# Row buffers of 4096 bytes and pads in a transformer block's kernel

## The chip, the cores and the metric

The kernel runs on one core of one Trainium2 chip, as one program. The metric is device time in microseconds from launch to end, the median of three runs: 1248.03 (1245.07 to 1248.34). One further execution was profiled and took 1247.24 us; every time read from the trace belongs to it.

## What is computed

One layer of a block with 1024 latent tokens and 256 context tokens of width 1024. The reference, cut:

```python
px = modulate(rms_norm(x, g_pre_mix), sh_m, sc_m) @ w_in       # 1024 tokens
pc = modulate(rms_norm(ctx, g_pre_mix), csh_m, csc_m) @ w_in   # 256 context tokens
att_x = window_attention(qx, kx, vx, kc, vc, sink)             # 8 query heads, 2 key heads, band 128
h_ml_x, _, _ = mlstm_bidir(xq, xk, xv, xg, st_f, st_b)         # 4 heads, both directions
mix_x = concatenate([att_x, ml_x], -1) @ w_out
x = x + gt_m * rms_norm(mix_x, g_post_mix)
fx = (silu(h @ w_gate) * (h @ w_up)) @ w_ffn_out               # h: x normed, modulated; hidden 2816
x = x + gt_f * rms_norm(fx, g_post_ffn)
```

The shifts, scales and gates are products of a conditioning vector with the six parts of w_ada.

## The kernel before

All data is float32. A product of two float32 operands is made of three matmuls in the type float32r: each operand is split into a rounded part (hi, copied by ScalarE, L59) and the rest (lo, subtracted by VectorE, L60), and `mm3` (L68) issues hi·hi, hi·lo and lo·hi as lines 71 to 73. In the terms of the code the first operand of a matmul is the stationary one, loaded into TensorE as weights (PEld in the profile), and the second moves past it. The moving operand is mostly 512 columns wide, 2048 bytes of a partition; the stationary one 128 columns, 512 bytes.

The stages, with their times in the profiled execution:

- 0 to 50 us: shift and scale from w_ada (L209). Norm, transposition and split of the tokens begin here (`prep_a`, `prep_b`).
- 50 to 92: gates, attention values and the first mLSTM head (`s1`, slabs of 272 columns of w_in, moving operand w1, stationary hh, hl or ch, cl).
- 92 to 133: the other three mLSTM value heads (slabs of 384 columns, L392, moving w2). `gates` (L303) and `ml_weights` (L378) run beside it.
- 133 to 309: thirteen weight tiles of w_in (`tproj`, L427, lines 438, 439, 441; stationary th and tl in R, moving hh, hl). Convolutions, rotary, the remaining w_ada parts (`ada_rest`, L479; sums over the partitions L499, L505) and the mLSTM state steps (`state_step`, L531) run between them.
- 309 to 498: attention and mLSTM outputs, item by item after a written plan (L35, L36).
- 498 to 600: output projection row by row (`omm`, L883; stationary mh and ml, moving woh and wol in R), norms, transposition, split into b11 to b22.
- 600 to 1009: gate and up products. The 2816 hidden columns go in 22 steps p by a scheme of seven products for each two-by-two block (`fm`, L1163). Each product is 12 matmuls, so a step is 84. Products 1, 2 and 3 have b11, b21, b22 moving; products 6, 5, 7 and 4 have T2, T1, T3, T4 (tT in the profile), which lie in R.
- 1009 to 1245: down projection by the same scheme (`fmm`, L1434; both operands are in one buffer fo), 924 matmuls.

From L873 on the order of the instructions of each engine is written out by hand; before it a planner places them. All DMAs are issued from SP's queue, in program order.

**Where the buffers lie.** Pools are opened as a stack: one from the low end of each partition's memory, another (side right) from the high end. Their buffers follow each other with starts at multiples of 32 bytes, so the sizes fix where each begins. The function `R` (L119) hands out sixteen row buffers, r0 to r15, that many stages share; each is RW = 1032 floats, 4128 bytes, which is eight times 512 and 32 more. They lie in the order of their first use: r0 to r3, r8 to r13, r6, r4, r7, r14, r15, r5. The remainders of the starting addresses modulo 512, worked out from the sizes:

| buffers | remainder modulo 512 |
|---|---|
| hh, hl (tokens), later mix | 480 |
| r0 to r3 (ch, cl; states; woh, wol; T3) | 352, 384, 416, 448 |
| r8 to r13 | 480, 0, 32, 64, 96, 128 |
| r6, r4, r7, r14, r15, r5 | 160, 192, 224, 256, 288, 320 |
| th, tl (in r9, r10 and r11, r12) | 0, 32 and 64, 96 |
| V; av2 | 352; 0 |
| w1h, w1l (rows of 1088 bytes) | 256 or 0 |
| w2h, w2l | 0 |
| k2, qh and ql | 256, 320 |
| probabilities split for the values product (th_, tl_) | 0 |
| mh, ml; b11 to b22; wg; wS and w22; fo | 352 |

A slice of 128 or 512 columns begins a multiple of 512 bytes into its buffer, so it has the buffer's remainder. The rows of V and of the mLSTM states have 129 floats, 516 bytes, so their slices do not. A buffer that is opened over released ones waits for the last use of those that it overlaps (`reuse_waits="tile"`).

Of the kernel before, what the change touches and what calls it, by code (L numbers as in the profile page):

```python
# [9 lines left out]
F32 = mybir.dt.float32  # L10
F32R = mybir.dt.float32r
# [5 lines left out]
P = 128  # L17
# [13 lines left out]
NCONST = 576  # L31
VSIL, VCONV, VGML, VBADA, VGPM, VGPF = 0, 16, 28, 32, 64, 72
NVEC = 80
RW = 1032
PLAN_ML = "T0 q A0 A1 A2 A3 T1 T2 T3 M0 M1 T4 V0 N0 M2 V1 M3 M4 O z V2 w V3 s N1 x"  # L35
PLAN = "T0 q A0 A1 A2 A3 T1 T2 T3 N0 M0 T4 M1 M2 N1 M3 M4 O z l"  # L36

# [1 line left out]
def body(tc, x, ctx, vecs, bcv, bada, gqm, gqf, wada, ws1, ws2, wt, wout, wfi, wfo,  # L39
# [5 lines left out]
    def open_pool(name, bufs=1, side="left", space=None):  # L45
        kw = dict(name=name, bufs=bufs, reuse_waits="tile")
        if space is not None:
            kw["space"] = space
        else:
            kw["side"] = side  # L50
        p = tc.tile_pool(**kw)
        return p, p.__enter__()
# [32 lines left out]
    c = cp[1]  # L85
# [11 lines left out]
    hcol = c.tile([P, 2, KT], F32, name="hcol")  # L97
    sfc = c.tile([P, KT], F32, name="sfc")
    hfc = c.tile([P, KT], F32, name="hfc")
    dma(vec, vecs)  # L100
    pool.memset(epst, EPS)
    pool.memset(one, 1.0)
# [14 lines left out]
    rp = open_pool("R")  # L117

    def R(k, name, shape, dt=F32):  # L119
        t = rp[1].tile([P, RW], dt, name=name, tag=f"r{k}")  # L120
        n = int(np.prod(shape))
        v = t[:, 0:n]
        if len(shape) == 2:
            v = v.rearrange("p (a b) -> p a b", b=shape[1])
        elif len(shape) == 3:
            v = v.rearrange("p (a b c) -> p a b c", b=shape[1], c=shape[2])
        elif len(shape) == 4:
            v = v.rearrange("p (a b c d) -> p a b c d", b=shape[1], c=shape[2], d=shape[3])
        return v


    vp = open_pool("V")
    V = vp[1].tile([P, NT, 4, 129], F32, name="V")
    Vc = vp[1].tile([P, NC_, 4, 129], F32, name="Vc")
    av2 = vp[1].tile([P, NT + NC_, 4, 64], F32R, name="av2")
    G = vp[1].tile([P, 4, 16, 4], F32, name="G")
    pool.memset(V[:, :, :, 128:129], 1.0)
# [7 lines left out]
    hh = [htp[1].tile([P, 4, S], F32R, name=f"hh{i}") for i in range(2)]  # L145
    hl = [htp[1].tile([P, 4, S], F32R, name=f"hl{i}") for i in range(2)]
    ch = [R(i, f"ch{i}", (4, L), F32R) for i in range(2)]
    cl = [R(2 + i, f"cl{i}", (4, L), F32R) for i in range(2)]
    gp = open_pool("gcol")
    ucol = gp[1].tile([P, P], F32, name="ucol")  # L150
    emcol = gp[1].tile([P, P], F32, name="emcol")
    wkcol = gp[1].tile([P, P], F32, name="wkcol")
    decb = gp[1].tile([P, 64], F32, name="decb")
    a_d = tc.dram_tile([P, P], F32, name="a_d")
    w_d = tc.dram_tile([P, P], F32, name="w_d")
    p1 = open_pool("p1")
    q1 = p1[1]
    w1h = [q1.tile([P, 4, 272], F32R, name=f"w1h{i}") for i in range(2)]
    w1l = [q1.tile([P, 4, 272], F32R, name=f"w1l{i}") for i in range(2)]

    cs4 = q1.tile([P, KT, 4], F32R, name="cs4")
    cz4 = q1.tile([P, KT, 4], F32, name="cz4")
    split(cs4[:, :, 0:2], cs4[:, :, 2:4], csil)
# [13 lines left out]
    def prep_a(i):  # L177

        j = i - NT
        xt = xts[i] = R(4 + i % 4, f"xt{i}", (D,))  # L180
        xd[i] = dma(xt, x[i * P:(i + 1) * P] if i < NT else ctx[j * P:(j + 1) * P])
        hraw[i] = R((12, 13, 8, 9, 10, 11)[i % 6], f"hraw{i}", (KT, P))
        act.activation(hraw[i].rearrange("p a b -> p (a b)"), xt, AF.Square, accum_out=st[:, i:i + 1])
        rms_r(st[:, 10 + i:11 + i], st[:, i:i + 1])
        pool.tensor_scalar(xt, xt, st[:, 10 + i:11 + i], 1.0, MUL, MUL)
# [23 lines left out]
    for sec in (1, 0):  # L209
# [30 lines left out]
        for q in range(2):  # L240
            t = (hcol, scol)[sec][:, q]
# [157 lines left out]
    akp = open_pool("ak")  # L399
    k2 = [akp[1].tile([P, S + L], F32R, name=f"k2_{g}") for g in range(2)]  # L400
    c1t = [akp[1].tile([P, 2, 129], F32, name=f"c1t{d}") for d in range(2)]
    p2 = open_pool("p2")
    q2 = p2[1]
    mk = [R(4 + i, f"mk{i}", (S,)) for i in range(2)]
# [10 lines left out]
    def T(i, name):  # L415
        return q2.tile([P, S], F32, name=name, tag=f"s{i}")
# [169 lines left out]
    for j, name in enumerate(TILES):  # L586
# [5 lines left out]
        i = int(name[-1]) if name[-1].isdigit() else 0  # L592
# [4 lines left out]
        elif name == "ak":  # L597
# [5 lines left out]
            for a, b, w, dst in ((kr, ks, S, slice(0, S)), (kc[:, 0:L], kc[:, L:2 * L], L, slice(S, S + L))):  # L603
                t = th[64:P] if w == S else kc[64:P, 2 * L:3 * L]
# [7 lines left out]
        elif name.startswith("aq"):  # L612
            t = T(0, f"aq{i}")
# [3 lines left out]
        else:  # L617
            t = R(14 if i == 3 else 15, "so", (S,))
# [23 lines left out]
        if 0 <= j - 3 < 9:  # L642
            s_ = j - 3
            if s_ >= 1 and s_ % 2 == 1:
                k = (s_ - 1) // 2
# [12 lines left out]
    mix = [mixt[:, n] for n in range(NT)]  # L658
    atp = open_pool("att")
    qa = atp[1]  # L660

    def bank():
        return pb.tile([P, 4, P], F32, name="pt", tag="pt", bufs=3)
# [787 lines left out]
    for p in range(4, HT):  # L1451
# [41 lines left out]
        else:  # L1493
            X4 += two_banks()
            t = pb.tile([P, D], F32, name="fx2", tag="s", bufs=2)
# [85 lines left out]
    for s_ in range(1, 8):  # L1581
        q0 = (s_ - 1) * NJ
        KL = 4 if s_ == 7 else 2
        if s_ == 2:
            t = pb.tile([P, D], F32, name="fy0", tag="s", bufs=2)
# [121 lines left out]
```

## Time and profile before

| what | us |
|---|---|
| median of three runs | 1248.03 |
| profiled execution | 1247.24 |
| its span, first to last instruction | 1245.4 |
| TensorE busy (PE) | 1205.8 |
| VectorE busy (DVE) | 799.9 |
| ScalarE busy (ACT) | 580.1 |
| GpSimd busy (POOL) | 204.0 |

In the trace a row of a group has the line, the engine, the operation, what is written and read by the program's names (numbers left out), the shape, the count, the busy time in us and the mean of one in ns, and after the last bar the idle time before them with what ended it. The records of neighbouring matmuls overlap: a record reaches from a matmul's start to the end of its last result. The rate is the step from one start to the next.

### The profile page before, as it was taken

What the parts mean: (1) busy time and instruction counts of PE and PEld (TensorE: products, weight loads), DVE (VectorE), ACT (ScalarE), POOL (GpSimd) and SP (SyncE); (2) the same over time, 40 slices, a digit from 0 to 9 for tenths busy, and PEclk for the clock granted to TensorE, in tenths of its full rate; (3) what the DMA queues carried; (4) which work ended last, traced back from release to release, by engine and by line L of the source; (5) the groups of instructions that cost most, each with busy time, mean ns of one, the idle gap of its engine ahead of it and who ended that gap; (6) DMA issues with size and microseconds to landing.
All of it is one profiled execution on the core that took longest, in us unless ns stands there. A gap on an engine that the chain in (4) does not pass through costs nothing.

```text
span 1245.4 us, 16232 instructions
## 1 busy us (share of the span) xinstructions
PE 1205.8 (97%) x5859; PEld 971.7 (78%) x5859; DVE 799.9 (64%) x1375; ACT 580.1 (47%) x1111; POOL 204.0 (16%) x245
## 2 busy tenths in 40 slices
PE   7889999999999998999899999999999999999997
PEld 1779887877777786888678888888888878888885
DVE  3882268763877787355867677767776655554566
ACT  3754533111666796677633333333333325434542
POOL 0752401244644475000000000000000000000000
PEclk9899999999999999999999999999999999999999
DMA  8532855655422320522033465665644547665853
GB/s 310 173 123 73 300 164 152 186 147 197 121 85 86 114 74 9 203 81 72 17 104 140 162 220 189 216 237 191 216 144 169 180 160 268 203 212 187 308 172 118
DMA packets 90952, 201.78 MB, mean 162 GB/s; under 512 B 9076, under 2 KB 29940, under 8 KB 89464
## 3 DMA queue, kind: packets, MB, share of 16 engines
q1 hardware_dynamic: 90872, 200.74, 48.1%
q8 instruction: 46, 0.75, 0.2%
q14 instruction: 34, 0.28, 0.1%
HBM read 149.32 MB, written 50.73 MB: 161 GB/s over the span
## 4 chain that ended last, share of the span: by engine, by line
PE 74%; DVE 9%; DMA 7%; ACT 4%; POOL 2%; issue 2%; SPq 1%; DVEq 0%; POOLq 0%; ACTq 0%
PE xv L72 7%; PE xv L71 7%; PE xv L73 7%; PE pt L72 5%; PE pt L71 5%; PE pt L73 5%; PE pt L704 2%; PE pt L703 2%; PE pt L804 2%; DMA wb<-in_wada 2%; PE t L438 2%; PE t L441 2%; PE t L439 2%; PE s L774 1%; PE op L71 1%
## 5 line engine op out<-in xcount | busy, mean ns | idle before, releaser
L60 DVE TENSOR_TENSOR fo<-fr,fo 128x1024 fp32r<-128x1024 f32 x77 | 92.7, 1222 | 71.4 <-ACT fo L59 68.4
L59 ACT CAST fo<-fr 128x1024 fp32r<-128x1024 f32 x77 | 79.6, 1051 | 74.0 <-PE pt L73 36.5
L438 PE MATMUL t<-hh,th 128*128 128x512 f32 x208 | 83.4, 401 | 0.9 <-ACT cr L455 0.9
L439 PE MATMUL t<-hl,th 128*128 128x512 f32 x208 | 82.6, 397 | 0.0
L59 ACT CAST wS<-wr 128x512 fp32r<-128x512 f32 x88 | 54.1, 622 | 57.9 <-PE pt L73 38.0
L60 DVE TENSOR_TENSOR wS<-wr,wS 128x512 fp32r<-128x512 f32 x88 | 60.4, 688 | 20.8 <-ACT wS L59 20.7
L71 PE MATMUL xv<-tT,wS 128*128 128x512 f32 x168 | 67.7, 403 | 3.7 <-ACT tT L1079 2.0
L441 PE MATMUL t<-hh,tl 128*128 128x512 f32 x208 | 68.6, 394 | 0.0
L72 PE MATMUL xv<-tT,wS 128*128 128x512 f32 x168 | 67.6, 402 | 0.0
L73 PE MATMUL xv<-tT,wS 128*128 128x512 f32 x168 | 66.6, 397 | 0.3 <-DVE wS L60 0.3
L489 DVE SCALAR_TENSOR_TENSOR acc<-wb,csil,acc 128x1024 f32<-128x1024 f32 x24 | 34.4, 1433 | 39.4 <-DMA wb<-in_wada 39.2
L438 PEld LDWEIGHTS t<-hh,th 128*128 128x128 f32 x208 | 39.1, 188 | 10.1 <-ACT cr L455 1.3
L940 DVE TENSOR_TENSOR wr<-wr 128x512 f32<-128x512 f32 x66 | 45.5, 689 | 1.5
L439 PEld LDWEIGHTS t<-hl,th 128*128 128x128 f32 x208 | 39.1, 188 | 8.4 <-issue 1.2
L1191 ACT ACTIVATE es<-es 128x512 f32<-128x512 f32 x22 | 13.9, 632 | 67.6 <-DVE es L943 67.6
L441 PEld LDWEIGHTS t<-hh,tl 128*128 128x128 f32 x208 | 38.2, 188 | 8.5 <-issue 1.0
L71 PE MATMUL op<-woh,mh 128*128 128x512 f32 x112 | 44.7, 399 | 0.0
L72 PE MATMUL op<-wol,mh 128*128 128x512 f32 x112 | 44.2, 394 | 0.0
L73 PE MATMUL op<-woh,ml 128*128 128x512 f32 x112 | 44.1, 394 | 0.0
L774 PE MATMUL s<-k,qh 128*128 128x256 f32 (+1 forms) x128 | 41.5, 335 | 1.9 <-ACT so L620 1.0
L71 PE MATMUL pt<-fo 128*128 128x512 f32 x110 | 42.8, 389 | 0.0
L72 PE MATMUL pt<-fo 128*128 128x512 f32 x110 | 42.8, 389 | 0.0
(982 smaller groups left out, 3498.1 us busy)
## 6 DMA issues: line engine op xcount, KB each, us to landing
wr<-in_wfi SPq DMA_DIRECT2D x44, 512.0 KB, 5.0
wb<-in_wada SPq DMA_DIRECT2D x24, 512.0 KB, 4.1
s_d<-a SPq DMA_DIRECT2D x22, 512.0 KB, 6.5
bt<-in_wfo SPq DMA_DIRECT2D x44, 256.0 KB, 4.0
tb_d<-bt SPq DMA_DIRECT2D x11, 1024.0 KB, 3.9
fr<-s_d SPq DMA_DIRECT2D x44, 256.0 KB, 3.5
fr<-tb_d SPq DMA_DIRECT2D x44, 256.0 KB, 4.6
fr<-a_d SPq DMA_DIRECT2D x33, 256.0 KB, 4.3
```

Source lines behind the costliest of these rows:

```text
L59: act.copy(hi, raw)
L60: dve.tensor_tensor(lo, raw, hi.bitcast(F32), SUB)
L71: pe.matmul(ps, a[0], b[0], start=first, stop=False, **kw)
L72: pe.matmul(ps, a[0], b[1], start=False, stop=False, **kw)
L73: pe.matmul(ps, a[1], b[0], start=False, stop=last, **kw)
L438: pe.matmul(o, wh[:, kt], m[0], start=f, stop=False)
L439: pe.matmul(o, wh[:, kt], m[1], start=False, stop=False)
L441: pe.matmul(o, wl[:, kt], m[0], start=False, stop=l)
L489: dve.scalar_tensor_tensor(a, t, csil[:, kt, 0:1], a, MUL, ADD)
L703: pe.matmul(pv[:, j, :], qp_[r, d, j, :], cs[r, j, :], start=True, stop=False)
L774: pe.matmul(o, qh[:, h, :], k2[g][:, kc], start=True, stop=False)
L940: dve.tensor_tensor(out, a, b, SUB)
```

## The change

R's buffers have 1152 floats (4608 bytes) where k is under 4, else 1024 (4096 bytes), in place of 1032. Five buffers that nothing reads or writes are added, with 32, 88, 64, 112 and 80 floats. w1h and w1l get rows of 384 floats of which 272 are used, and decb gets 128 floats of which 64 are used. No instruction is added, removed or reordered in the text.

```diff
-RW = 1032
...
+    c.tile([P, 32], F32, name="pad")
...
-        t = rp[1].tile([P, RW], dt, name=name, tag=f"r{k}")
+        t = rp[1].tile([P, 1152 if k < 4 else 1024], dt, name=name, tag=f"r{k}")
...
     Vc = vp[1].tile([P, NC_, 4, 129], F32, name="Vc")
+    vp[1].tile([P, 88], F32, name="padv")
...
-    decb = gp[1].tile([P, 64], F32, name="decb")
+    decb = gp[1].tile([P, 128], F32, name="decb")[:, 0:64]
...
-    w1h = [q1.tile([P, 4, 272], F32R, name=f"w1h{i}") for i in range(2)]
-    w1l = [q1.tile([P, 4, 272], F32R, name=f"w1l{i}") for i in range(2)]
-
+    w1h = [q1.tile([P, 4, 384], F32R, name=f"w1h{i}")[:, :, 0:272] for i in range(2)]
+    w1l = [q1.tile([P, 4, 384], F32R, name=f"w1l{i}")[:, :, 0:272] for i in range(2)]
+
+    q1.tile([P, 64], F32, name="padw")
...
     c1t = [akp[1].tile([P, 2, 129], F32, name=f"c1t{d}") for d in range(2)]
+    akp[1].tile([P, 112], F32, name="pada")
...
     qa = atp[1]
+    qa.tile([P, 80], F32, name="padq")
```

## The prediction

> **What bounds the kernel now.** I read the page first, then the busy times by stage, then the groups of instructions with shapes kept apart, and then single starts of matmuls. The page says that TensorE is the engine to look at:
>
> ```profile
> PE 1205.8 (97%) x5859; PEld 971.7 (78%) x5859; DVE 799.9 (64%) x1375; ACT 580.1 (47%) x1111; POOL 204.0 (16%) x245
> PE 74%; DVE 9%; DMA 7%; ACT 4%; POOL 2%; issue 2%; SPq 1%; DVEq 0%; POOLq 0%; ACTq 0%
> ```
>
> PE is busy 97% of the span and is three quarters of the chain that ended last. The stretches by stage (PE alone; busy time and number of matmul records) say where that holds:
>
> ```profile
> core 0: us, PE busy (x), PEclk, DMA share, GB/s
> 92.00:133.00 41.00, 41.00 (x241) 1.00 0.32 110
> 133.00:163.60 30.60, 29.90 (x153) 1.00 0.85 289
> 163.60:309.00 145.40, 144.71 (x760) 1.00 0.54 163
> 309.00:498.00 189.00, 181.18 (x1082) 0.99 0.28 85
> 498.00:600.00 102.00, 101.78 (x474) 1.00 0.32 114
> 690.00:980.00 290.00, 290.00 (x1260) 1.00 0.56 192
> 1060.00:1140.00 80.00, 80.00 (x354) 1.00 0.67 210
> ```
>
> From 163.6 to 309 (the weight tiles, L427), from 498 to 600 (output projection, L1097) and from 690 to 980 (gate and up products, L1451) PE never stops, at a granted clock of 1.00. There a matmul that is shorter by some ns shortens the program by the same ns. So the question is what one 512-column matmul takes, and whether its buffers have a part in it. The groups, shapes kept apart (count, busy us, mean ns of one):
>
> ```profile
> L438 PE MATMUL t<-hh,th 128*128 128x512 f32 x208 | 83.4, 401 | 0.9 <-ACT cr L455 0.9
> L439 PE MATMUL t<-hl,th 128*128 128x512 f32 x208 | 82.6, 397 | 0.0
> L441 PE MATMUL t<-hh,tl 128*128 128x512 f32 x208 | 68.6, 394 | 0.0
> L71 PE MATMUL xv<-tT,wS 128*128 128x512 f32 x168 | 67.7, 403 | 3.7 <-ACT tT L1079 2.0 <-ACT eu L1193 1.5
> L72 PE MATMUL xv<-tT,wS 128*128 128x512 f32 x168 | 67.6, 402 | 0.0
> L73 PE MATMUL xv<-tT,wS 128*128 128x512 f32 x168 | 66.6, 397 | 0.3 <-DVE wS L60 0.3
> L71 PE MATMUL op<-woh,mh 128*128 128x512 f32 x112 | 44.7, 399 | 0.0
> L72 PE MATMUL op<-wol,mh 128*128 128x512 f32 x112 | 44.2, 394 | 0.0
> L73 PE MATMUL op<-woh,ml 128*128 128x512 f32 x112 | 44.1, 394 | 0.0
> L71 PE MATMUL pt<-fo 128*128 128x512 f32 x110 | 42.8, 389 | 0.0
> L71 PE MATMUL xv<-b11h,wg 128*128 128x512 f32 x84 | 32.9, 392 | 0.0
> ```
>
> All have one shape, and they fall into two classes. Products of two buffers outside R (fo with fo, b11h with wg) take 389 to 392 ns; products with an operand in R (th and tl, tT, woh and wol) take 394 to 403. By the sizes in the section on the kernel, both operands of the first class begin 352 bytes past a multiple of 512. In the second class they differ: hh at 480 with th at 0 or 32 and tl at 64 or 96; tT and woh at all multiples of 32 against weights at 352.
>
> A mean is not a rate, since records overlap, so I take the step from start to start. In the down projection (26 steps between these two) and in one step of the gate product (24 steps, all with tT):
>
> ```profile
> 1099.93 0.39 PE L71 MATMUL pt<-fo 128*128 128x512 f32 x1
> ...
> 1105.83 0.39 PE L73 MATMUL pt<-fo 128*128 128x512 f32 x1
> ```
> ```profile
> 719.91 0.40 PE L71 MATMUL xv<-tT,wS 128*128 128x512 f32 x1
> ...
> 725.48 0.40 PE L71 MATMUL xv<-tT,wS 128*128 128x512 f32 x1
> ```
>
> The first is 5.90 us over 26 steps, 226.9 ns each; the second is 5.57 us over 24, 232.1 ns. The output projection (46 steps) and a run of the weight tiles (20 steps) are like the second:
>
> ```profile
> 539.02 0.40 PE L72 MATMUL op<-wol,mh 128*128 128x512 f32 x1
> ...
> 549.70 0.39 PE L73 MATMUL op<-woh,ml 128*128 128x512 f32 x1
> ```
> ```profile
> 260.31 0.40 PE L438 MATMUL t<-hh,th 128*128 128x512 f32 x1
> ...
> 264.96 0.40 PE L438 MATMUL t<-hh,th 128*128 128x512 f32 x1
> ```
>
> 10.68/46 is 232.2 ns and 4.65/20 is 232.5 ns. So a matmul with unlike remainders costs 5.2 to 5.6 ns more than one in the first run. One more thing has to be seen. After a break an aligned run is slow too:
>
> ```profile
> 1145.95 0.39 PE L73 MATMUL pt<-fo 128*128 128x512 f32 x1
> 1146.33 0.50 PE L71 MATMUL fx<-fo 128*128 128x512 f32 x1
> 1146.67 0.40 PE L72 MATMUL fx<-fo 128*128 128x512 f32 x1
> ...
> 1148.76 0.39 PE L72 MATMUL pt<-fo 128*128 128x512 f32 x1
> ...
> 1150.12 0.39 PE L72 MATMUL po<-fo 128*128 128x512 f32 x1
> ```
>
> After the late start at 1146.33, nine steps take 2.09 us (232 ns each), and only then six take 1.36 us (226.7 each). I read it as a rhythm of the two reads (the running matmul's and the next one's weight load) that settles after some nine matmuls when both begin alike, and never does when they do not. A break thus costs 9 x 5.5, some 50 ns, of what alignment gives.
>
> **The change part by part.** The pads (128 bytes in const, 352 in V, 256 in p1, 448 in ak, 320 in att) hold nothing: no instruction, no wait. With the buffers of R at 4096 or 4608 bytes, w1 rows at 1536 and decb at 512, every operand named above comes to begin at 480, as hh, hl and mix do already: 352 + 128 is 480; R is 67,584 bytes, 132 x 512; V, Vc and the pad are 20,992, 41 x 512. All buffers from V on lie 1,664 to 3,040 bytes higher, and I find each stage's buffers over the same released ones as before, save a few that were released earlier. So I cost the waits on reused memory at nothing. The longest of them is hidden by attention's end: the first x row is loaded into space that the last values product (L815) frees, in both layouts.
>
> ```profile
> SPq L977 <- PE po L815: 27.7, 1, 27.7
> ```
>
> Were such a cover gone, the price would be one more wait of the size of PE's own at a change of stage, 0.9 to 2.0 us in the rows of L438 and xv's L71.
>
> - Gate and up products: 290.00 us for 1260 records, of which some 1.7 began before the stretch, is 230.5 ns a matmul, over all 84 of a step p (48 with tT, 36 already alike). At 226.7 that is 3.8 ns less. Some 20 of the 22 steps run without a stop: 1680 x 3.8 = 6.4 us. The bounds are 5 (breaks stay) and 7 (all 1848).
> - Output projection: a row is 48 matmuls; 5.5 x 48 less one break is 0.21 us, for seven rows 1.5 us. The first row is made in short pieces and gives nothing. Bounds 0.5 and 1.8.
> - Weight tiles from 163.6: about 500 matmuls of 512 columns at 5.8 ns are 2.9 us. But a state step (L531) breaks the run four times a tile, nine times over, and the reductions (L499, L505) three times: up to 39 breaks of 50 ns, 2.0 us. I take 1.4, between 0.9 and 2.9, since some breaks stand close together.
> - Before 163.6 most is lost. PE waits there for something else:
>
> ```profile
> 156.96 4.10 DMA wb<-in_wada
> ...
> 163.13 0.58 ACT cr L455
> ```
>
> The row of L438 above has 0.9 us of idle time from it. The copy that frees the PSUM bank hangs on a chain of wada's load and the DVE queue behind it, so what PE saves between 112 and 163 makes this wait longer. In the slabs before it (240 of 272 columns and 240 of 384) PE also waits for DVE and ACT up to 92. I take 0.5 us, of bounds 0 and 1.5.
> - Attention: only the scores (L774, 256 matmuls, 256 or 384 columns) come from unlike to like; at up to 5.5 ns they give 0 to 1.4 us, and most stand in runs of two or eight. I take 0.2. Its value products (L814) begin alike already, and those of L703 and L704 have rows of 516 bytes, which no pad can align.
> - Down projection: alike before and after, nothing.
> - DVE, ACT and POOL work on the same shapes at moved addresses; I cost that at nothing, since in the gate and down stages above PE is busy throughout and waits for none of them. If it slowed a split there, a wait of PE on it would show, which is the half case below.
>
> The sum is 6.4 + 1.5 + 1.4 + 0.5 + 0.2 = 10.0 us. The profiled execution took 1247.24 (span 1245.4 and 1.8 around it), so it would take 1237.2; it lies 0.8 below the median of the runs, 1248.03, so the forecast is 1238.0. A measurement of this kernel can tell some 0.3%, 3.7 us, from no change.
>
> [...]
>
> **The rivals.**
>
> *Half of it* (about 5.5 us, 1242.5): runs settle in the gate product alone, or PE's faster pace meets a split or a load that is then late. For it: DVE is busy 64% of the span, and breaks stand close in the weight tiles. Against it: in the gate stage no wait of PE shows for 290 us.
>
> *No change* (1248): the 5.5 ns come from the neighbours of these matmuls, not from addresses. What speaks for it is that products with R run where DVE and ACT are split many ways; against it that b11h with wg, in the same stage, interleaved with them, has 392 where tT has 397 to 403, and that all three lines of t are slow though their neighbours vary. [...]
>
> *Slower*: what counts is not that the two remainders are equal but that they are 352. Attention has a pair at remainders 0 and 0:
>
> ```profile
> 352.41 0.40 PE L814 MATMUL po<-th__3177,av 128*128 128x512 f32 x1
> 352.65 0.39 PE L815 MATMUL po<-tl__3178,av 128*128 128x512 f32 x1
> ```
>
> Its step is 240 ns, not 227. If 480 were no better than 0, the products that are fast now (924 of the down projection, 36 x 20 of the gate stage) would go to 232.3, the mean of the three unlike runs: 1644 x 5.6 is 9.2 us more, 1257. Against it: that pair follows a break, where the aligned run above was as slow, and hh at 480 is no slower than tT elsewhere. It decides as soon as fo's settled step is over 230.
>
> **How the numbers follow.** The forecast has 0.70; half of it 0.15; no change 0.09; slower 0.06. Faster by over 0.3% are the first two, 0.85. The terms' bounds together give 6.4 to 14.6; all at one end at once is unlikely, so 7 to 13, and with the runs' own spread (1245.07 to 1248.34) and the half case the range is 1233 to 1244.
>
> **What would show it.** Right: th, tT and woh groups at 389 to 392 like fo, a gate stretch at 227 ns a matmul, fo unchanged, a longer wait of L438 on cr, and breaks that still start slow. Wrong: fo over 390 (the slower case), t and tT still at 395 or more (no change), or new waits of PE on ACT or DVE in the gate stage (half).

## The result and the profile after

The changed kernel took 1240.04 us (median of 6 runs, 1238.05 to 1241.05), the kernel before 1247.51 in the same comparison (6 runs, 1245.07 to 1249.96). The ratio is 0.9936, with a 95% interval of 0.9921 to 0.9950: 7.5 us or 0.6% faster. The forecast was 1238.0. The profiled execution of the changed kernel took 1238.05 us (span 1236.3); the one before took 1247.24 (1245.4).

All line numbers have moved: mm3's are now 70 to 72, the weight tiles' 441, 442 and 444. The page's busy row, and its chain row by engine (its shares add up to 75%, since this chain is followed back only to 307 us; so PE's 65% is not to be set beside the 74% of before):

```profile
PE 1193.3 (97%) x5859; PEld 971.0 (79%) x5859; DVE 798.9 (65%) x1375; ACT 579.9 (47%) x1111; POOL 205.1 (17%) x245
PE 65%; DVE 4%; ACT 3%; POOL 1%; DMA 1%; issue 1%; DVEq 0%; ACTq 0%
```

PE has 12.5 us less to do; the others have what they had (the split of fo on DVE takes 1222 ns in both). The groups by shape (count, busy us, mean ns, idle before):

```profile
L441 PE MATMUL t<-hh,th 128*128 128x512 f32 x208 | 82.6, 397 | 1.7 <-ACT cr L458 1.7
L442 PE MATMUL t<-hl,th 128*128 128x512 f32 x208 | 82.2, 395 | 0.0
L444 PE MATMUL t<-hh,tl 128*128 128x512 f32 x208 | 68.3, 393 | 0.0
L70 PE MATMUL xv<-tT,wS 128*128 128x512 f32 x168 | 66.9, 398 | 4.9 <-ACT tT L1083 2.3 <-ACT eu L1197 1.6 <-DVE es L947 1.0
L71 PE MATMUL xv<-tT,wS 128*128 128x512 f32 x168 | 66.3, 395 | 0.0
L70 PE MATMUL op<-woh,mh 128*128 128x512 f32 x112 | 44.3, 395 | 0.0
L71 PE MATMUL op<-wol,mh 128*128 128x512 f32 x112 | 43.7, 390 | 0.0
L70 PE MATMUL pt<-fo 128*128 128x512 f32 x110 | 42.8, 389 | 0.0
L70 PE MATMUL xv<-b11h,wg 128*128 128x512 f32 x84 | 32.8, 391 | 0.0
```

Every group of this list with R went down, by 1 to 7 ns, and those that were alike before stayed within 1. Of these rows only the second matmul of the output projection comes down to fo; t, xv and the first of op still have breaks in them (and xv a stretch at half clock, below). Steps from start to start show it without the overlap. Here are the matmuls that the prediction used: 24 steps with tT, 46 of the output projection, 20 of the weight tiles:

```profile
715.71 0.39 PE L70 MATMUL xv<-tT,wS 128*128 128x512 f32 x1
...
721.15 0.39 PE L70 MATMUL xv<-tT,wS 128*128 128x512 f32 x1
...
535.22 0.40 PE L71 MATMUL op<-wol,mh 128*128 128x512 f32 x1
...
545.68 0.40 PE L72 MATMUL op<-woh,ml 128*128 128x512 f32 x1
...
258.24 0.40 PE L441 MATMUL t<-hh,th 128*128 128x512 f32 x1
...
262.83 0.39 PE L441 MATMUL t<-hh,th 128*128 128x512 f32 x1
```

5.44/24 is 226.7 ns (232.1 before), 10.46/46 is 227.4 (232.2), 4.59/20 is 229.5 (232.5, the last with a break ahead of it). The stretches by stage, in the same view as before:

```profile
163.60:309.00 145.40, 143.88 (x770) 1.00 0.56 165
686.25:976.25 290.00, 290.00 (x1281) 1.00 0.56 194
1060.00:1140.00 80.00, 80.00 (x353) 1.00 0.62 194
```

The 290 us of the gate stage now hold 1281 matmuls instead of 1260. Less the 1.7 that began before the stretch, as in the prediction, that is 226.7 ns each after 230.5. Both kernels run the same matmuls in the same order, so a stage can be measured from the start of one matmul to the start of the same matmul in another kernel (named by the times of before; us):

| profiled execution | 133 to 164 | weight tiles, 164 to 309 | attention, to 499 | output projection, to 601 | start of gate stage, to 640 | gate and up, to 998 | their end, to 1029 | down, to 1236 |
|---|---|---|---|---|---|---|---|---|
| before | 30.89 | 145.41 | 189.42 | 102.30 | 38.93 | 358.23 | 30.17 | 207.17 |
| after | 31.65 | 143.82 | 188.80 | 100.95 | 40.67 | 352.40 | 29.69 | 207.17 |

The last gate products stand among the first products of the down projection, up to 1029 us; from there on all operands are in fo. The starts at 640 and 1029 us, before and then after:

```profile
640.14 0.39 PE L73 MATMUL xv<-tT,w 128*128 128x512 f32 x1
...
1028.54 0.39 PE L71 MATMUL pt<-fo 128*128 128x512 f32 x1
...
637.27 0.39 PE L72 MATMUL xv<-tT,w 128*128 128x512 f32 x1
...
1019.37 0.39 PE L70 MATMUL pt<-fo 128*128 128x512 f32 x1
```

So the gate stage gave 6.3 us (388.40 to 382.10; 5.8 of it up to 998), the weight tiles 1.6 and the output projection 1.35. Two stretches became longer: 133 to 164 by 0.8, which the prediction had announced, and the start of the gate stage by 1.7, which it had not.

### The profile page after: what moved, and what is told of

Its sections match the earlier page's. It is cut to its first block, busy times and chain, and to the rows that moved or that the text cites. A ratio compares the mean times of both kernels' runs of the same rounds, so it can differ in the third digit from the quotient of the medians.

```text
span 1236.3 us, 16232 instructions
## 1 busy us (share of the span) xinstructions
PE 1193.3 (97%) x5859; PEld 971.0 (79%) x5859; DVE 798.9 (65%) x1375; ACT 579.9 (47%) x1111; POOL 205.1 (17%) x245
## 4 chain that ended last, share of the span: by engine, by line
PE 65%; DVE 4%; ACT 3%; POOL 1%; DMA 1%; issue 1%; DVEq 0%; ACTq 0%
PE xv L72 7%; PE xv L71 7%; PE xv L70 7%; PE pt L72 5%; PE pt L71 5%; PE pt L70 5%; PE pt L708 2%; PE pt L707 2%; PE pt L808 2%; PE fx L70 1%; PE op L72 1%; PE op L70 1%; PE op L71 1%; PE fx L72 1%; PE fx L71 1%; PE s L778 1%
## 5 line engine op out<-in xcount | busy, mean ns | idle before, releaser
L59 DVE TENSOR_TENSOR fo<-fr,fo 128x1024 fp32r<-128x1024 f32 x77 | 92.7, 1222 | 71.2 <-ACT fo L58 60.8
L441 PE MATMUL t<-hh,th 128*128 128x512 f32 x208 | 82.6, 397 | 1.7 <-ACT cr L458 1.7
L70 PE MATMUL xv<-tT,wS 128*128 128x512 f32 x168 | 66.9, 398 | 4.9 <-ACT tT L1083 2.3
L72 PE MATMUL xv<-tT,wS 128*128 128x512 f32 x168 | 66.2, 394 | 0.3 <-DVE wS L59 0.3
L71 PE MATMUL xv<-tT,wS 128*128 128x512 f32 x168 | 66.3, 395 | 0.0
L441 PEld LDWEIGHTS t<-hh,th 128*128 128x128 f32 x208 | 39.1, 188 | 10.4 <-ACT cr L458 2.1
L72 PE MATMUL pt<-fo 128*128 128x512 f32 x110 | 42.8, 389 | 0.0
L71 PE MATMUL pt<-fo 128*128 128x512 f32 x110 | 42.8, 389 | 0.0
L70 PE MATMUL pt<-fo 128*128 128x512 f32 x110 | 42.8, 389 | 0.0
```

What stands on the lines that cost most here:

```text
L59: dve.tensor_tensor(lo, raw, hi.bitcast(F32), SUB)
L70: pe.matmul(ps, a[0], b[0], start=first, stop=False, **kw)
L71: pe.matmul(ps, a[0], b[1], start=False, stop=False, **kw)
L72: pe.matmul(ps, a[1], b[0], start=False, stop=last, **kw)
L441: pe.matmul(o, wh[:, kt], m[0], start=f, stop=False)
```

## The experiments

**Three kernels in which the operands begin elsewhere.** Their edits are made to the changed kernel. The theory on record is that the two starts of a product have to be equal modulo 512; its rivals, that the value itself counts (the slower case), and that only a change from matmul to matmul hurts. In the first kernel the buffers that follow the first pad (R and those opened after it from the low end) go back to 352 together, and hh, hl and mix stay at 480:

```
-    c.tile([P, 32], F32, name="pad")
```

> The change without its first pad (32 floats in const): R and everything opened after it begin at 352, only hh and hl stay at 480. Theory 1 (a product is fast when both operands begin at one remainder, whichever it is): output, gate and down stages as in the changed kernel (steps of 226.7 ns after settling), the weight tiles (difference 128) at 230 to 233 again, their stage 1.6 us longer, in all some 1241.5. Theory 2 (only some remainders are good, 352 and 480 among them): the same. Theory 3 (a constant difference between the operands does no harm, only a remainder that changes from one matmul to the next does): the weight tiles keep the gain, 1240.

In the second these buffers begin at 448, and in the third those of R alone at 416:

```
-    c.tile([P, 32], F32, name="pad")
+    c.tile([P, 24], F32, name="pad")
```

> The first pad has 24 floats in place of 32: R and everything after it begin at 448, a multiple of 64, where 352 and 480 are odd multiples of 32; hh and hl stay at 480. Theory 1: as the run with 352, some 1241.5, settled steps of fo 226.7. Theory 2: fo, b11h and tT at 232, 394 ns a record in place of 389, and the whole at 1253 or more. Theory 3: 1240.

```
-    c.tile([P, 32], F32, name="pad")
+    c.tile([P, 16], F32, name="pad")
...
+    rp[1].tile([P, 16], F32, name="padr")
```

> R's buffers at 416 (first pad of 16 floats, and 16 floats behind R), everything else at 480 as in the changed kernel. Every product with an operand in R then has one and the same difference of 64, and no moving remainder changes within t and op; within the gate stage it changes between products only. Theory 1: gate stretch back to 230 to 231 ns a matmul, output stage 102.3, weight tiles 145.4, in all 1247. Theory 3: the gain stays, 1240.

Measured: 1242.22 us (4 runs; ratio 0.9948, 0.9933 to 0.9963), 1241.88 (4 runs; 0.9940, 0.9923 to 0.9957) and 1249.24 (10 runs; 1.0013, 1.0002 to 1.0024), the kernel before at 1247.83 (13 runs).

| | 133 to 164 | 164 to 309 | to 499 | to 601 | to 640 | to 998 | to 1029 | down, to 1236 |
|---|---|---|---|---|---|---|---|---|
| low at 352 | 32.31 | 145.61 | 189.43 | 100.92 | 40.71 | 352.40 | 29.74 | 207.18 |
| low at 448 | 32.94 | 147.34 | 189.48 | 100.88 | 40.50 | 352.40 | 29.73 | 207.19 |
| R at 416 | 31.16 | 144.37 | 189.31 | 102.77 | 38.97 | 359.10 | 30.25 | 207.13 |

The gate stage takes 352.40 us and the down projection 207.2 at 352, 448 and 480 alike: the value does not count, and the slower case is out. (In the profile at 448 the granted clock was 0.5 from 163.6 to 167.0 us; the section on the missing 2.5 us takes this up.) With R at 416 against 480 everywhere, a difference that never changes, the gains of the gate stage and the output projection are gone. The row of its gate stage:

```profile
690.00:980.00 290.00, 290.00 (x1257) 1.00 0.56 192
```

1257 matmuls, even fewer than the 1260 before. So it is the difference of the two starts that counts.

**The disputed cost by itself.** A kernel that leaves the layer out and copies x to the output runs 23 segments of 96 matmuls of 512 columns, with the operands of each at chosen starts and all other engines idle:

```
+            pe.matmul(bk, wb[:, w + j * P:w + j * P + P], mb[:, m + j * P:m + j * P + 512],
+                      start=k == 0, stop=k == n - 1)
...
+    seg("segB", (32,), (32,))
...
+    seg("segI", (256,), (0,))
```

> Not the layer: the kernel computes nothing of the reference, it only runs 23 segments of 96 matmuls of 512 columns with chosen starting addresses, nothing beside them on the other engines, four transpositions between segments; its output is a copy of x. A record's mean less 162 ns is the step. Theory 1: segments A, B, C (equal remainders 0, 32, 224) at 389 to 390; D to O (differences of 32 to 480, by the moving or the stationary operand) at 393 to 397; P to S (a remainder that alternates) as slow; T, U, V (equal, broken every 24, 12, 6 matmuls) ever closer to the slow ones. Theory 2: A slow, B and C fast or the reverse. Theory 3: D to O fast, P to S slow. If the neighbours on other engines made the difference, all segments are alike.

Its groups: starts of both at 32 (B), moving operand ahead by 32 (D), 64 (E), 128 (G), 192 (H) and 256 bytes (I), stationary ahead by 256 (O), and a break of four transposes after every 12 matmuls with equal starts (U) and with 32 bytes between them (W):

```profile
L67 PE MATMUL segW<-mb,wb 128*128 128x512 f32 x96 | 24.3, 402 | 0.0
L67 PE MATMUL segU<-mb,wb 128*128 128x512 f32 x96 | 24.1, 400 | 0.0
L67 PE MATMUL segD<-mb,wb 128*128 128x512 f32 x96 | 22.6, 396 | 0.0
L67 PE MATMUL segH<-mb,wb 128*128 128x512 f32 x96 | 22.6, 395 | 0.0
L67 PE MATMUL segG<-mb,wb 128*128 128x512 f32 x96 | 22.5, 395 | 0.0
L67 PE MATMUL segE<-mb,wb 128*128 128x512 f32 x96 | 22.2, 392 | 0.0
L67 PE MATMUL segI<-mb,wb 128*128 128x512 f32 x96 | 22.1, 390 | 0.0
L67 PE MATMUL segB<-mb,wb 128*128 128x512 f32 x96 | 22.1, 390 | 0.0
L67 PE MATMUL segO<-mb,wb 128*128 128x512 f32 x96 | 22.0, 390 | 0.0
```

The 390 ns of aligned products and the 395 or 396 of most others are here without any neighbour, so the no-change rival's reason (DVE and ACT beside it) falls. With a break every twelve matmuls, 2 of the 6 ns between unlike and equal starts are left (U and W). And a difference of 256 is as good as none, in either operand. In steps from start to start, after the first ten of a segment, by moving start minus stationary start: 0 and 256 have 226.7 ns, 64 and 320 have 228.9 and 228.8, 128 and 384 have 232.3 and 232.2, and 32, 96, 192, 448 and 480 have 233.3 or 233.4. This repeats with 256, and the three kernels above fall in the same order: the mean of the weight tiles' steps under 250 ns is 228.8 in the changed kernel (equal, breaks included), 229.7 with th at 416 (hh ahead by 64), 232.4 at 352 (by 128) and 233.2 at 448 (by 32). With R at 416 the gate stage has the moving operand 64 behind, which is 192: 233.3, slower than the mixture of before.

Segments B and D differ in nothing but a start address, and D's step is 6.7 ns longer (233.4 after 226.7); segment I, with 256 between its starts, has 226.7 again. So what the step takes depends on both operands' starts together; why it does is not shown.

**256 in the layer.** R moves to 224 (two of its sixteen buffers to 480), all else stays at 480:

```
-    c.tile([P, 32], F32, name="pad")
+    c.tile([P, 96], F32, name="pad")
...
-        t = rp[1].tile([P, 1152 if k < 4 else 1024], dt, name=name, tag=f"r{k}")
+        t = rp[1].tile([P, 1088 if k < 4 else 1024], dt, name=name, tag=f"r{k}")
...
+    rp[1].tile([P, 64], F32, name="padr")
```

> The 16 buffers of R moved so that 14 of them begin at remainder 224 modulo 512 and two at 480, while hh, hl, mix and everything above R stay at 480: nearly all products with R now differ by 256 bytes, none by another amount; 512 bytes less memory in all, same instructions in the same order. Theory A (what counts is the start address modulo 256): the gate stage from fi1 to the down products 352.4 us and the t stage 143.8 us, as with the change, 1240 in all. Theory B (modulo 512, as the change's words have it): gate 358 to 359, t 145 to 146, out 102.5, so 1248 to 1249, like the kernel that put R at 416.

It took 1240.65 us (5 runs; ratio 0.9934, 0.9908 to 0.9960). The row of its gate stage, to be set beside the one with R at 416:

```profile
690.00:980.00 290.00, 290.00 (x1281) 1.00 0.56 196
```

1281 again; gate stage 352.40, weight tiles 143.74, output projection 100.96. The remainder that counts is modulo 256; the change's 512 does more than it needs.

**Where the missing 2.5 us went.** The sum of the terms was 10.0 us and the medians gave 7.5. Three more kernels start from the changed one. The first edit gives tag cr two buffers (at all three places of that tag; one is shown), so that the copy that frees PE's PSUM bank at 163 us need not wait for a convolution on DVE:

```
-            rw = q2.tile([P, S + 2], F32, name="cr", tag="cr")
+            rw = q2.tile([P, S + 2], F32, name="cr", tag="cr", bufs=2)
```

> The changed kernel with two buffers for cr in place of one, which lets the copy that frees the PSUM bank before 163 us run without waiting for DVE's third conv step; a few instructions around it change places. Theory A (the saving before 163 was lost in the wait of the products' t on the copy, 1.7 us): that wait falls to under 0.3 us and the time by 1.4 to 1.7 us, to about 1238.5. Rival: DVE's queue behind wada's loads makes the next slab late instead; the wait moves to another line and the time stays at 1240.

The second puts nine matmuls into PE's wait for tT at the start of the gate stage, into a bank that a later product (k = 5) starts anew:

```
+            if p == 0:
+                zb[0] = bank().rearrange("p a b -> p (a b)")
+                for i in range(9):
+                    pe.matmul(zb[0], wops[2]["11"][:, 0, i % 4], bop("11")[i % 4][0], start=True, stop=True)
             mm_fi(X, w["S2"], top("T2"), False)
...
-            zb[p] = bank().rearrange("p a b -> p (a b)")
+            if p:
+                zb[p] = bank().rearrange("p a b -> p (a b)")
```

> The changed kernel with nine matmuls that leave nothing (their bank is overwritten by the next product's start) put into PE's wait of 2.3 us ahead of the first product fm(0,6) of the gate stage. Theory A (that wait halves the granted clock for the next 3.4 us, and the chain through ACT and DVE then takes it over): no step of 427 ns after it, the stretch from 601 to 640 falls from 40.7 to about 39.0, and the time by 1.7 us, to about 1238.3. Rival (the half clock only lies beside the ACT and DVE chain from the output projection's end, which alone sets the end): the matmuls run at full clock, the stretch stays within 0.4 us and the time at 1240.

The third has both:

> Both of the two edits before on the changed kernel: two buffers for cr and the nine matmuls. If each lost piece is what it is taken for, the two add up: 1236.5 to 1237, which is what the sum of the terms had promised (10 us below the kernel before). If either rival holds, 1238 to 1240.

They took 1240.12, 1238.97 and 1239.95 us (5 runs each; the kernel before 1248.57; ratios 0.9931, 0.9928, 0.9930, each with about 0.0018 to either side). Later, on one chip, the changed kernel and the second edit ran again:

> The changed kernel again, unedited, beside the next one on the same chip: 1240.0, some 7.5 us under the kernel before. If half clock periods after waits differ from execution to execution, single runs differ by steps of about 1.5 us.

> The changed kernel with the nine matmuls in PE's wait ahead of the gate stage, again. Theory A (the half clock period there comes in about two of three executions of the changed kernel and costs 1.6 us): about 1.0 to 1.1 us under the changed kernel in this call, 1239.0. Rival (no part of the time): the same as the changed kernel to 0.3 us.

They took 1240.52 us (6 runs, 1238.55 to 1244.30; ratio 0.9938, 0.9920 to 0.9956) and 1237.96 us (5 runs, 1237.13 to 1240.31; 0.9918, 0.9902 to 0.9933).

| | 133 to 164 | 164 to 309 | to 499 | to 601 | to 640 | to 998 |
|---|---|---|---|---|---|---|
| two cr | 29.67 | 149.37 | 189.14 | 100.98 | 39.20 | 352.39 |
| nine matmuls | 31.86 | 145.24 | 190.93 | 100.98 | 39.30 | 352.40 |
| both | 29.79 | 148.63 | 190.83 | 100.92 | 39.26 | 352.40 |
| changed kernel again | 32.46 | 145.29 | 191.32 | 100.93 | 40.94 | 352.41 |
| nine matmuls again | 32.44 | 143.73 | 189.37 | 100.95 | 39.33 | 352.39 |

Start with the start of the gate stage. The windows view of the changed kernel, first the whole stretch, then the 4.4 us after PE's wait for tT (third column from the right: the granted clock):

```profile
596.37:637.04 40.67, 34.76 (x136) 0.96 0.18 58
601.98:606.40 4.42, 4.42 (x12) 0.62 0.00 0
```

Twelve matmuls in 4.42 us: for 3.4 us the granted clock was a half, and each step took 427 ns. PE had waited 2.3 us for tT, after 2.0 in the kernel before: the chain on ACT and DVE that it waits for (norm, transposition and split of the last rows) begins behind a row of the projection and takes 31.8 us in both (574.60 to 606.37 before, 570.21 to 601.98 here), so what PE saves beside that chain only lengthens the wait. With the nine matmuls in the wait (the timeline of the second of the two runs):

```profile
600.82 2.20 PE L1179 MATMUL pt<-b11h,wg 128*128 128x512 f32 x9
603.26 0.50 PE L70 MATMUL xv<-tT,wS 128*128 128x512 f32 x1 [0.24 <-ACT tT L1083]
...
604.77 0.40 PE L72 MATMUL xv<-tT,wS 128*128 128x512 f32 x1
```

the wait is 0.24 us, the steps behind it are at full speed, and in all three runs with this edit the stretch takes 39.3 us instead of 40.4 to 40.9. (In the second of the two runs a half period came at 612.9 us, beside a chain on DVE, and the stretch took 39.33 all the same.) Theory A for this wait holds, with one thing added: the kernel with two cr waited 2.3 us as well, met no half clock there, and has 39.20. So the half clock is a chance of the execution: it came in five of the six profiled executions with a wait of 2.3 us. Over all runs the nine matmuls gave 1239.1 on the mean of ten, the changed kernel 1240.5 on the mean of twelve; 1.4 us with an interval of about -0.1 to 2.9. This version has the lowest mean, but that it is faster in the whole time is not clear of chance.

Two buffers for cr did take the wait at 163 away, 2 us between 133 and 164. But the weight tiles then took 5.5 us more, so the time stayed at 1240.12 and not at the 1238.5 of theory A. Its waits of PE there (in total, how many, the longest), and the windows around one of them:

```profile
PE pu L545 <- DVE mkc L541: 3.6, 3, 1.4
```
```profile
205.34:208.75 3.41, 1.97 (x18) 1.00 0.60 165
208.75:212.16 3.41, 3.41 (x9) 0.50 0.81 251
```

PE now waits 3.6 us, in three pieces, for DVE to scale keys (L541), and the clock was halved behind it. That is the rival on record: the wait moved to another line. The kernel with both edits shows the same (148.63), so the two edits did not add up to the 1236.5 to 1237 that was hoped for.

The changed kernel run again says how much of this is chance. Its program is the same; this execution took 1242.97 us, not 1238.05. PE's wait at 163, and the windows before and behind it:

```profile
PE t L441 <- ACT cr L458: 2.5, 1, 2.5
```
```profile
160.50:163.60 3.10, 0.62 (x3) 1.00 0.36 114
163.60:167.02 3.42, 3.42 (x9) 0.50 0.79 248
```

The wait was 2.5 us long, not 1.7, and the clock was halved here, and again at 443.5, 607.3 and 617.6 us. Why this wait differs between executions is not shown; the nine-matmul kernel had 2.5 us here too, with no half clock behind it (133 to 309: 176.2 us, against 177.8 here). In the first profile of the changed kernel one such period lay between 50 and 1230 us (603.1), in the one before two (311.7 and 615.4, the latter beside a DVE chain, where it cost nothing).

**What halves the clock.** A kernel that leaves the layer out lets PE wait on DVE 35 times, for 1.05 to 3.83 us, between stretches of 41 to 49 matmuls:

```
+        dve.tensor_scalar(tmp, bk[:, 0:256], 0.0, None, MUL)
+        for _ in range(m):
+            dve.tensor_tensor(tmp, tmp, raw[:, 0:256], MUL)
+        dve.tensor_tensor(gm[:, 0:256], tmp, raw[:, 0:256], ADD)
```

> A kernel of its own (it leaves the layer out and returns rows of x): stretches of 41 to 49 matmuls of 128x512 whose operands begin alike, 35 times broken by a wait of PE on a chain of one to seven short DVE operations, so waits from about 0.7 to 3 us, five of each. Theory A (the granted clock is set anew every 3.41 us on a grid that runs by itself, to half where PE was idle for about half of the 3.41 us before): waits under 1.5 us never halve it, waits of 2.3 us do in two of three cases by where they fall on the grid, waits of 3 us always; each half period costs 8 matmuls x 200 ns, 1.6 us. Rival (any wait over some 2 us halves the clock, wherever it falls): the cases part cleanly by the wait's length.

All its half periods (granted clock 0.5) are 3.41 or 6.83 us long and begin at multiples of 3.413 us from one another. After waits of 1.05 and 1.53 us there was none (0 of 10). After 1.99 us there were 4 of 5, after 2.45 us 1 of 5, after 2.91 us 5 of 5, after 3.37 us 3 of 5, after 3.83 us 5 of 5. Two waits of 2.45 us, in windows of that grid:

```profile
415.81:419.22 3.41, 3.40 (x16) 1.00 0.00 0
419.22:422.64 3.42, 0.98 (x4) 1.00 0.00 0
422.64:426.05 3.41, 3.41 (x9) 0.50 0.00 0
...
224.66:228.08 3.42, 2.35 (x11) 1.00 0.00 0
228.08:231.49 3.41, 2.03 (x9) 1.00 0.00 0
231.49:234.90 3.41, 3.41 (x17) 1.00 0.00 0
```

The first wait lies in one window, PE is busy for 0.98 us of it, and the next window is at half clock. The second is shared by two windows, and nothing follows. Among all of them, a window at full clock in which PE was busy for 0.42 or less was followed by a half one, and with 0.44 or more by none (one at 0.42: busy for 1.43 of 3.42 us from 64.23 us on, then 3.41 us at 0.50). So theory A holds in kind, and the rival falls, since 1.99 us halved more often than 2.45. Theory A's odds (two of three at 2.3 us, all at 3) are not confirmed: 1 of 5 at 2.45 and 3 of 5 at 3.37, though five waits of a length are few. In the layer the boundary is less sharp: between 50 and 1225 us half periods followed busy shares of 0.27 (ahead of 163.6 us in the changed kernel again) to 0.58 (ahead of 208.75 us with two cr), and one window at 0.47 was followed by none (601.3 us, two cr).

The layer has the same grid: in the kernel before, the half periods at 311.66 and 615.45 us begin 303.79 us apart, 89 times 3.413. It is not tied to the program's start: in the two profiled executions of the changed kernel the grids lie 0.9 us apart, counted from the first instruction (half periods at 603.1 in one and 607.3 us in the other).

## Why the prediction was right, and where its sizes were off

The mechanism held for matmuls of 512 columns, with 256 in the place of 512. Products whose operands begin alike settle at 226.7 ns, others do not (up to 233.4; those 64 ahead come near, at 228.9), the value of the remainder is indifferent (352.40 us for the gate stage at 352, 448 and 480), the cost is there without DVE and ACT (records of 396 ns after 390), and breaks start slow anew (400 with one every twelve matmuls). That the cause is a rhythm of two reads stays the author's reading; no run shows it. fo stayed at 389, after 640 us no new wait of PE appeared in the gate stage, and L441's wait on cr grew as announced. By its terms:

- Gate and up products: 6.3 of 6.4 us, from 640 to 1029 us, where the last of them ends: 3.8 ns on each of 1666 (forecast: 1680).
- Weight tiles: 1.6 of 1.4, in the executions where the wait at 163 halved nothing; 0.1 or 0.2 in the others.
- Before 163.6: the term of 0.5 us can't be told from scatter. The stretch from the first matmul to the one at 50 us took 41.6 to 45.1 us in these kernels; from 50.7 to 133.2 us it was 82.5 us before, 81.5 and 82.4 in the two profiled executions after. The slabs with w2 (384 columns) gave nothing: their 179 unbroken steps with hh or hl took 173.7 ns on the mean before, with starts 32 bytes apart, and 173.9 after, with equal ones (175.9 in the kernel with 352, 128 apart). So the 5 to 6 ns of 512 columns were not there to be gained. What the prediction feared is there: the wait on cr grew from 0.9 to 1.7 us, and to 2.5 in another execution of the same program.
- Attention 0.2: 0.6, within what executions of the changed program differ by (188.80 and 191.32).
- Down 0: 0, 207.17 us from 1029 us on in both.
- Output projection: 1.5 was forecast and 1.35 came, but in the profiled execution none of it was left at 640 us. Here a step of the prediction was too simple: "From 163.6 to 309 (the weight tiles, L427), from 498 to 600 (output projection, L1097) and from 690 to 980 (gate and up products, L1451) PE never stops", so that a shorter matmul shortens the program by as much. Within the stage that is so; but at its end PE waits for ACT and DVE, and the prediction asked what is late next only ahead of 163.6, and had no term for the clock. The wait took 0.2 us of the 1.35. The half clock behind it took 1.5: from the first matmul with tT to 640 us it was 33.77 us before and 35.29 after, but 33.82 in the kernel with two cr, where the clock stayed full. From 499 to 640 the kernel before took 141.23 us, the changed one 141.62, the one with two cr 140.18, and with nine matmuls in the wait 140.28.

In the two profiled executions the sum is 9.1 us by spans, against 10.0; but 1.8 of it lie ahead of 133 us, where executions scatter, so that it comes so near is in part luck. In the medians it is 7.5, since the profiled execution of the changed kernel was the shortest of its six. The difference goes with half clock periods behind PE's waits, some 1.5 us each. The two waits on the way were 0.9 and 2.0 us and are now 1.7 to 2.5 and 2.3: a part of what PE saves ahead of a wait lengthens it. That the changed kernel has more such periods than the one before in general is argued, not shown: of the kernel before there is one profile, with two of them. That these periods make the runs differ is shown for the profiled ones; for the runs without a profile there is only their mean granted clock to go by: of twelve of the changed kernel, the four at 0.994 took 1238.1 to 1239.7 us, the five at 0.991 or less 1240.0 to 1244.3.

## What to carry to other kernels

In long unbroken runs of 512-column matmuls, let the stationary and the moving operand begin at one remainder modulo 256 bytes; in the 23 segments unlike starts cost up to 6.7 ns on 226.7 in every step (3%), and behind a break in the down projection nine steps took 232 ns each before 226.7 came back. At 384 columns starts 32 bytes apart cost nothing that could be gained (173.7 ns, 173.9 with equal ones). Pads do it without an instruction, but count the gain only in stages that end on PE itself: where PE then waits for another engine, the wait can grow by a part of what was saved (0.2 of 1.35 us at the gate stage). A wait of PE of 2 us or more can cost twice, because the clock may be halved behind it (after 1.99 us in four of five cases, after 1.53 in none; behind the wait of 2.3 us ahead of the gate stage it took 1.5 us more); nine matmuls into a bank that is overwritten anyway cut that wait to 0.24 us and kept the clock full behind it.

## What was not expected of the hardware

In the 23 segments of 512 columns the period is 256 bytes, not 512, and the cost is graded: 226.7 ns at a difference of 0, 228.9 at 64, 232.3 at 128, 233.3 at 32 or 192. With the moving operand's start alternating by 32 bytes against a fixed stationary one the step is 230.0, half of what the constant difference adds; alternating by 256 it is 226.7. Why 64 ahead is cheap and 64 behind is not stays open. The clock was halved behind waits as short as 1.99 us, in periods of 3.413 us or twice that, on a grid that is not tied to the program's start (0.9 us apart in two executions of one program). And at 384 columns starts 32 bytes apart cost nothing that shows (173.7 ns, 173.9 with equal ones).
